# Hybrid decoder layer on one core: the low weight parts of the per-head products made on Pool instead of VectorE

## Chip, cores and metric

One NeuronCore of a Trainium2 chip runs the whole kernel. The metric is the device time of one execution in microseconds (us). The names of the engines are those of the profile: PE is TensorE (matmul), DVE is VectorE, ACT is ScalarE, POOL is GpSimd, SP is SyncE, which here only issues DMAs.

## What is computed

A hybrid decoder layer over 512 tokens of width 2048, in float32: an attention branch with forget gates (8 heads of 128) and an RWKV-7 branch (16 heads of 64, handled in 8 pairs), each gated, merged, projected and normalised.

```python
h = _rmsnorm(x, norm_gain)
u = h @ w_in                                  # 2048 x 12488
q, k, v, z_a, f_logit = _split(u_fox, ...)    # 4 x 1024 + 8 columns
o_a = _fox_attention(q, k, v, log_f) * silu(z_a)
r, kr, vr, z_b, w_down, a_down = _split(_token_shift(u_rwkv), ...)
y = _rwkv7_scan(r, decay, k, v, kk, kk * a)   # S = S*w + (S@-kk) b^T + v k^T per token
o_b = (groupnorm(y) + bonus) * silu(z_b)
m = sigmoid(g_a) * (o_a @ w_proj_fox) + sigmoid(g_b) * (o_b @ w_proj_rwkv)
out = _rmsnorm(x + m @ w_out, final_norm_gain)
```

## The kernel before

Every large product is done in three matmuls of a short float format: the operand is split into a high part (rounded) and a low part (the rest), and high x high, low x high and high x low are added up in PSUM. The activations' parts hhi and hlo are made once and stay in SBUF. The weights stream through.

A weight tile of 2048 x 128 is cut into four pieces of 128 x 512 values (256 KB). Each piece goes through four steps. SP issues its load into one of four raw buffers (`load_raw`, L236, the DMA on L239). ACT makes the high part whi by a copy that rounds (L266). Another engine makes the low part wlo = raw - whi (L267, and L263 for the first four pieces). PE uses the piece in twelve matmuls of 512 columns (`product`, L278, through `mm`, L127). There are four buffers each of whi and wlo. `next_piece` (L242) hands out piece i and writes down the loads up to piece i+4 and the splits up to piece i+2, so PE works some pieces behind the splits. A raw buffer is loaded again only when the wlo of the piece in it has been made; SP waits for that on its own queue, in the order of the program.

The pieces have names: ad for one LoRA input, k, r, z, v for the RWKV pairs, fq, fk, fv, fz for the attention heads, g for the gates, p for the projections, o for the output. The first letter decides in the changed line.

Time falls into three parts. Up to about 40 us the input is normalised and transposed. From 40 to about 990 us (the heads' stage) the products k, r, z, v of eight RWKV pairs and fq, fk, fv, fz of eight heads run as one main stream on PE, and the rest of the heads' work is woven between them. After that come gates, projections and the output product, a steady stream of matmuls. PE's and SP's instructions stand in the order of the program (`manual_schedule`, L154): the main stream advances a clock that counts PE's work alone, and a worker (`rwkv_front`, `rwkv_back`, `rwkv_chain`, `fox_head`) gets its next step when the clock has passed the delay of its last one (LAG, L52). The order on DVE, ACT and POOL is chosen by the framework when the program is built, by priority and an estimate of when operands are ready; `high_priority(offset=HW)` (L265) puts the splits ahead of what stands up to 150 instructions before them. At run time each engine works through its queue strictly in order.

Of the workers' steps the argument needs these. In `rwkv_back` DVE inverts small triangular blocks by 31 steps of a multiply (Wt, L641 through the helper at L482, both operands in SBUF) and a reduction (W, L642), one after the other; I call this the substitution loop. The attention heads' softmax stands among its last steps on DVE, and ACT's exponent (pr, L798) waits for the row maximum that DVE makes (fst, L796, L797). The loop's result goes out by SP to DRAM and back (w_d, L646 to L654), DVE transposes it (A, L658) and PE multiplies with it (gp, L675). `shift` (L443 to L448) takes an RWKV product out of PSUM by ACT and DVE, which frees one of the two PSUM banks of the main stream. In `rwkv_front` POOL makes two steps: a (L532) and kn = kn * a (L547, seen at L482), and DVE's split of rkk (L552, seen at L426) writes a buffer that this POOL step reads. POOL also copies AV (L705), clears parts of SV (L594) and issues the DMAs that store ob_d and oa_d (L771, L834).

Of the kernel before, what the change touches and what calls it, by code (L numbers as in the profile page):

```python
# [9 lines left out]
F32 = mybir.dt.float32  # L10
F32R = mybir.dt.float32r
AF = mybir.ActivationFunctionType
ALU = mybir.AluOpType
# [42 lines left out]
def hybrid_layer(  # L56
# [7 lines left out]
    V, S, G, PE = nc.vector, nc.scalar, nc.gpsimd, nc.tensor  # L64
# [177 lines left out]
    def next_piece():  # L242


        i = used[0]
        used[0] += 1
        while len(raws) < min(i + (RAWS + 1 if i > 3 else 4), len(pieces)):
            raws.append(load_raw(*pieces[len(raws)]))
        split_pieces(i + (3 if i > 3 else 1))
        got = parts[i]  # L250
        parts[i] = None
        return got

    def split_pieces(n):
        while len(parts) < min(n, len(pieces)):
            j = len(parts)
            name, srcs, nk, M = pieces[j]
            raw = raws[j]
            whi = wpool.tile([P, nk, M], F32R, tag="whi", bufs=4, name=f"whi_{name}")
            wlo = wpool.tile([P, nk, M], F32R, tag="wlo", bufs=4, name=f"wlo_{name}")  # L260
            if j < 4:
                G.tensor_copy(whi, raw)
                G.tensor_tensor(wlo, raw, whi.bitcast(F32), ALU.subtract)  # L263
            else:
                with tc.high_priority(offset=HW):  # L265
                    S.activation(whi, raw, AF.Copy)  # L266
                    V.tensor_tensor(wlo, raw, whi.bitcast(F32), ALU.subtract)  # L267
            parts.append((whi, wlo))


# [75 lines left out]
    for hf in range(2):  # L346
        t = slice(256 * hf, 256 * hf + 256)
        for j in range(0, KC + AHEAD, 2):
            if j < KC:
                turn(hf, j)  # L350
            if hf == 0 and j % 4 == 0 and j < KC:
                wd_w.append(next_piece())
                if j == 0:
                    for tb in range(2, 4):
                        for h2 in range(2):
                            load_x(nc.sync, tb, h2)
                    load_params()
            if hf == 0 and j in (SQ2, SQ3):
                norm_rows(2 if j == SQ2 else 3)
            if j < AHEAD:  # L360
                continue
            for kk in range(j - AHEAD, j - AHEAD + 2):
                whi, wlo = wd_w[kk // 4]
                mm(ps_wd[0:MW, t], whi[:, kk % 4, :], hhi[:, kk, t], start=(kk == 0), stop=False)
                mm(ps_wd[0:MW, t], whi[:, kk % 4, :], hlo[:, kk, t], start=False, stop=False)
                mm(ps_wd[0:MW, t], wlo[:, kk % 4, :], hhi[:, kk, t], start=False, stop=(kk == KC - 1))
            if hf == 1 and j - AHEAD in (4, 8, 12):
                split_pieces(4 + (j - AHEAD) // 4)
# [634 lines left out]
    for n in range(4):  # L1003
        pss = banks(n)
        for kk in range(KC if n < 3 else KC // 2):
            whi, wlo = next_piece()
# [55 lines left out]
```

## Time and profile before

| what | value |
|---|---|
| three runs | 1672.08, 1672.97, 1675.00 us; median 1672.97 us |
| the profiled execution's own time | 1676.68 us |
| its span, first to last instruction | 1674.8 us |
| busy over the span | PE 97%, DVE 57%, ACT 42%, POOL 5% |
| mean granted clock of PE | 0.993 |

Busy time alone does not tell what a change is worth. A busy PE can still have a queue that waited a moment before, and an engine that is half idle can be late at the few points where PE needs it. So the rows further down show first where PE stood still, and who released it, and then the durations of the operations that the change moves.

### The profile page before, as it was taken

The page shows a single profiled execution, that of the slowest core. Times are in us where ns is not written, and L with a number is a line of the kernel's source. Part 1 is how long each engine was busy: PE and PEld are TensorE (multiplying, and loading weights), DVE is VectorE, ACT ScalarE, POOL GpSimd, SP SyncE. Part 2 cuts the span into 40 slices and gives each one's busy share as a digit, 9 for nine tenths or more (in the row PEclk, how much of TensorE's full clock was granted, in tenths as well). Part 3 has the DMA queues.
Part 4 walks back from the last instruction along what each step waited for, and adds up shares of the span by engine and source line. Part 5 has one row for each costly group of instructions (what it writes and reads, how often), then busy time and mean ns, then how long its engine had stood idle before and what let it go on. Part 6 is the DMA issues. An engine that isn't in the chain of part 4 may idle for free.

```text
span 1674.8 us, 23424 instructions
## 1 busy us (share of the span) xinstructions
PE 1628.9 (97%) x8506; PEld 1332.3 (80%) x8506; DVE 958.0 (57%) x2005; ACT 710.4 (42%) x1453; POOL 83.6 (5%) x149
## 2 busy tenths in 40 slices
PE   6998998999999999999999999999999999999998
PEld 6887876778878778788788788888888888888886
DVE  6468587786877777678668454222224333353432
ACT  7544354474464464553744444222223222243322
POOL 3010001000000000010000000000000000001110
PEclk9999998999999999999999999999999999999999
DMA  5342423333333324334334244335334333343422
GB/s 167 97 107 69 105 61 90 98 87 86 90 96 98 99 70 111 86 78 104 85 86 115 76 123 118 95 98 148 94 96 148 97 95 98 98 160 117 138 83 101
DMA packets 287978, 170.24 MB, mean 102 GB/s; under 512 B 38790, under 2 KB 270830, under 8 KB 287222
## 3 DMA queue, kind: packets, MB, share of 16 engines
q1 hardware_dynamic: 284358, 156.13, 35.4%
q0 software_dynamic: 2064, 9.46, 1.5%
q10 hardware_dynamic: 1440, 3.15, 0.5%
q8 instruction: 67, 1.10, 0.3%
q14 instruction: 49, 0.40, 0.1%
HBM read 158.19 MB, written 10.50 MB: 101 GB/s over the span
## 4 chain that ended last, share of the span: by engine, by line
PE 83%; DVE 9%; ACT 3%; issue 2%; DMA 2%; SPq 1%; POOL 0%; DVEq 0%; ACTq 0%; POOLq 0%
PE u_g L135 20%; PE p L135 11%; PE o L135 10%; PE u_fq L135 6%; PE u_fk L135 5%; PE u_z L135 4%; PE u_fv L135 4%; PE u_k L135 4%; PE u_fz L135 4%; PE u_v L135 4%; PE u_r L135 2%; DVE Wt L482 2%; DVE W L642 1%; PE sc L135 1%; PE y L135 1%
## 5 line engine op out<-in xcount | busy, mean ns | idle before, releaser
L135 PE MATMUL u_g<-hhi,wlo_g 128*128 128x512 f32 x512 | 200.6, 392 | 0.0
L135 PE MATMUL u_g<-hhi,whi_g 128*128 128x512 f32 x512 | 200.4, 391 | 0.0
L135 PE MATMUL u_g<-hlo,whi_g 128*128 128x512 f32 x512 | 200.0, 391 | 0.0
L267 DVE TENSOR_TENSOR wlo_g<-raw_g,whi_g 128x512 fp32r<-128x512 f32 x128 | 88.4, 690 | 169.8 <-ACT whi_g L266 167.6
L266 ACT ACTIVATE whi_g<-raw_g 128x512 fp32r<-128x512 f32 x128 | 80.9, 632 | 228.1 <-PE u_g L135 115.1
L135 PEld LDWEIGHTS u_g<-hlo,whi_g 128*128 128x128 f32 x512 | 96.2, 188 | 20.3
L135 PEld LDWEIGHTS u_g<-hhi,wlo_g 128*128 128x128 f32 x512 | 96.2, 188 | 20.2
L135 PEld LDWEIGHTS u_g<-hhi,whi_g 128*128 128x128 f32 x512 | 96.2, 188 | 19.7
L482 DVE TENSOR_TENSOR Wt<-W,Lt 128x16 f32<-128x16 f32 (+30 forms) x248 | 101.0, 407 | 5.6
L267 DVE TENSOR_TENSOR wlo_p<-raw_p,whi_p 128x512 fp32r<-128x512 f32 x64 | 44.3, 693 | 103.3 <-ACT whi_p L266 103.3
L135 PE MATMUL p<-ohi,whi_p 128*128 128x512 f32 x256 | 101.0, 394 | 0.0
L135 PE MATMUL p<-ohi,wlo_p 128*128 128x512 f32 x256 | 100.4, 392 | 0.0
L135 PE MATMUL p<-olo,whi_p 128*128 128x512 f32 x256 | 99.6, 389 | 0.0
L266 ACT ACTIVATE whi_p<-raw_p 128x512 fp32r<-128x512 f32 x64 | 40.4, 631 | 121.9 <-PE u_g L135 120.3
L135 PE MATMUL o<-whi_o,mhi 128*128 128x512 f32 x224 | 87.3, 390 | 0.1
L135 PE MATMUL o<-wlo_o,mhi 128*128 128x512 f32 x224 | 87.2, 389 | 0.0
L135 PE MATMUL o<-whi_o,mlo 128*128 128x512 f32 x224 | 87.1, 389 | 0.0
L267 DVE TENSOR_TENSOR wlo_o<-raw_o,whi_o 128x512 fp32r<-128x512 f32 x56 | 42.6, 762 | 76.2 <-ACT whi_o L266 75.9
L642 DVE TENSOR_REDUCE W<-Wt 128x8 f32<-128x16 f32 (+30 forms) x248 | 72.4, 292 | 5.6
L266 ACT ACTIVATE whi_o<-raw_o 128x512 fp32r<-128x512 f32 x56 | 35.3, 631 | 83.6 <-PE o L135 79.3
L135 PE MATMUL u_fq<-hhi,whi_fq 128*128 128x512 f32 x128 | 53.7, 419 | 5.2 <-DVE z L448 5.2
L719 ACT ACTIVATE pre<-SV,E 64x64 f32<-64x64 f32 x112 | 38.6, 345 | 46.3 <-DVE SV L732 45.4
(352 smaller groups left out, 3924.3 us busy)
## 6 DMA issues: line engine op xcount, KB each, us to landing
raw_g<-in_w_in_dram SPq DMA_DIRECT2D x128, 256.0 KB
raw_o<-in_w_out_dram SPq DMA_DIRECT2D x56, 256.0 KB
raw_k<-in_w_in_dram SPq DMA_DIRECT2D x32, 256.0 KB
raw_r<-in_w_in_dram SPq DMA_DIRECT2D x32, 256.0 KB
raw_z<-in_w_in_dram SPq DMA_DIRECT2D x32, 256.0 KB
raw_v<-in_w_in_dram SPq DMA_DIRECT2D x32, 256.0 KB
raw_fq<-in_w_in_dram SPq DMA_DIRECT2D x32, 256.0 KB
raw_fk<-in_w_in_dram SPq DMA_DIRECT2D x32, 256.0 KB
```

What stands on the lines that cost most here:

```text
L135: PE.matmul(out, lhsT=lhsT, rhs=rhs, start=start, stop=stop, **kw)
L266: S.activation(whi, raw, AF.Copy)
L267: V.tensor_tensor(wlo, raw, whi.bitcast(F32), ALU.subtract)
L482: eng.tensor_tensor(o, a, b, op)
L642: V.tensor_reduce(W[:, :, i], tmp[:, :, 0:i + 1], AX.X, ALU.add)
L719: S.activation(pre[hs[q]], SV[hs[q], c, q, :], AF.Copy, scale=E1[hs[q], c, CH:CH + 1])
```

## The change

For pieces whose name begins with k, r, z, v or f, the subtraction that makes the low part is given to POOL (`G`) instead of DVE (`V`). These are the 256 pieces of the eight RWKV pairs and the eight heads. The four pieces of ad, and those of g, p and o, stay on DVE. Nothing else is edited; the orders on DVE, ACT and POOL are chosen anew when the program is built.

```diff
@@ -264,7 +264,7 @@
             else:
                 with tc.high_priority(offset=HW):
                     S.activation(whi, raw, AF.Copy)
-                    V.tensor_tensor(wlo, raw, whi.bitcast(F32), ALU.subtract)
+                    (G if name[0] in "krzvf" else V).tensor_tensor(wlo, raw, whi.bitcast(F32), ALU.subtract)
             parts.append((whi, wlo))
```

## Rows read from the trace of the kernel before

**Rows 1.** Busy time: stretch, length, PE, PEld, DVE, ACT, POOL, clock, DMA, GB/s
```profile
40.00:990.00 950.00, 925.16 (x5353) 751.59 (x5352) 690.13 (x1557) 473.55 (x1017) 47.79 (x71) 0.99 0.36 90
```

**Rows 2.** Waits of PE: tile and line, releaser, us in total, times, longest
```profile
PE gp L135 <- DVE A L658: 6.7, 2, 6.6
...
PE u_fq L135 <- DVE z L448: 5.2, 2, 4.5
PE bt L139 <- ACT BT L667: 3.3, 2, 1.7
...
PE st L135 <- ACT AV L725: 1.5, 3, 0.7
```

**Rows 3.** Timeline of PE at the two long waits: start, us, [idle before]
```profile
146.53 0.77 PE L135 MATMUL u_fq<-hhi,whi_fq 128*128 128x512 f32 x1 [4.54 <-DVE z L448]
147.09 0.63 PE L135 MATMUL u_fq<-hlo,whi_fq 128*128 128x512 f32 x1
147.52 0.63 PE L135 MATMUL u_fq<-hhi,wlo_fq 128*128 128x512 f32 x1
...
269.82 0.31 PE L135 MATMUL gp<-A,G 32*32 32x32 f32 x2 [6.59 <-DVE A L658]
```

**Rows 4.** Timelines of ACT, DVE and PE behind the seventh loop
```profile
796.07 0.40 ACT L798 ACTIVATE pr<-pr,fst 128x128 f32<-128x128 f32 x1 [4.91 <-DVE fst L797]
...
797.61 0.69 DVE L267 TENSOR_TENSOR wlo_r<-raw_r,whi_r 128x512 fp32r<-128x512 f32 x1 [0.36 <-PE u_r L135]
...
800.39 0.39 PE L135 MATMUL u_r<-hlo,whi_r 128*128 128x512 f32 x1
800.62 0.39 PE L135 MATMUL u_r<-hhi,wlo_r 128*128 128x512 f32 x1
```

**Rows 5.** The stretch behind the second wait, columns as in rows 1
```profile
270.00:275.00 5.00, 4.85 (x42) 3.89 (x41) 4.06 (x7) 1.60 (x3) 0.00 (x0) 0.54 0.06 16
```

**Rows 6.** Line 267: ns min/median/max, first and last start
```profile
L267 DVE TENSOR_TENSOR wlo_k<-raw_k,whi_k x32: 629/683/694, 40.8 to 786.9; 128x512 fp32r<-128x512 f32 x32
...
L267 DVE TENSOR_TENSOR wlo_fz<-raw_fz,whi_fz x32: 627/684/696, 178.7 to 982.7; 128x512 fp32r<-128x512 f32 x32
```

**Rows 7.** Waits of DVE as in rows 2, one line before low parts
```profile
DVE wlo_fv L267 <- ACT whi_fv L266: 15.8, 12, 4.5
```

**Rows 8.** Timeline of POOL: three of the eight kn steps
```profile
140.51 1.84 POOL L482 TENSOR_TENSOR kn<-kn,a 128x512 f32<-128x512 f32 x1 [5.99 <-DVE AR L545]
...
266.55 2.15 POOL L482 TENSOR_TENSOR kn<-kn,a 128x512 f32<-128x512 f32 x1 [5.33 <-DVE AR L545]
...
495.11 1.29 POOL L482 TENSOR_TENSOR kn<-kn,a 128x512 f32<-128x512 f32 x1 [5.13 <-DVE AR L545]
```

**Rows 9.** POOL groups: line, shapes, count, busy us and mean ns, idle before
```profile
L263 POOL TENSOR_TENSOR wlo_wd<-raw_wd,whi_wd 128x416 fp32r<-128x416 f32 x4 | 4.5, 1126 | 0.2
```

**Rows 10.** Timeline of DVE beside the first two kn steps
```profile
141.14 0.27 DVE L642 TENSOR_REDUCE W<-Wt 128x8 f32<-128x112 f32 x1
141.32 1.59 DVE L482 TENSOR_TENSOR AR<-r,E 128x512 f32<-128x512 f32 x1
...
263.22 0.63 DVE L482 TENSOR_TENSOR AR<-r,E 128x512 f32<-128x512 f32 x1
...
266.29 1.29 DVE L267 TENSOR_TENSOR wlo_fq<-raw_fq,whi_fq 128x512 fp32r<-128x512 f32 x2
268.73 0.69 DVE L426 TENSOR_TENSOR rlo<-rkk,rhi 128x512 fp32r<-128x512 f32 x1 [1.16 <-POOL kn L482]
```

**Rows 11.** Timeline of DVE in the output stage, beside four POOL multiplies
```profile
1537.87 3.47 DVE L267 TENSOR_TENSOR wlo_o<-raw_o,whi_o 128x512 fp32r<-128x512 f32 x2
```

**Rows 12.** Sums over eight loop stretches: all engines; Wt alone; line 267 alone
```profile
sum 303.00, PE 297.64 PEld 243.95 DVE 280.81 ACT 124.18 POOL 11.28; mean PE 37.21 PEld 30.49 DVE 35.10 ACT 15.52 POOL 1.41
...
sum 303.00, DVE 173.12; mean DVE 21.64
...
sum 303.00, DVE 60.46; mean DVE 7.56
```

## The prediction, made before the changed kernel was run

> **What bounds the kernel now.** I read the profile in three steps. First the busy time of the stage that the change touches: of the 950 us between 40 and 990 us PE is busy for 925.2, DVE for 690 and POOL for 48 [rows 1]. So PE sets the time, and all that any edit of DVE or POOL can give is what PE loses: 24.8 us of idle time, and a little clock. Second the list of PE's waits, which says who ended that idle time [rows 2]. Two sites are DVE's: 6.7 us in which gp waits for the transposed result of a substitution loop, and 5.2 us in which the main stream waits until a product has been taken out of PSUM. Five smaller lines, 11.7 us together, were ended by ACT (the first and the last of them are shown). No wait of PE for a low part is listed. Third the timeline at the two DVE sites [rows 3]: the waits are 4.54 us before 146.53 and 6.59 us before 269.82. Behind each of them PE runs slower for a while. After the first, matmuls start 0.43 us apart instead of 0.23 [rows 3, 4], twelve of them until 151.4 us, some 2.4 us. After the second, the granted clock is 0.54 over five microseconds, so mostly the lower level of 1.2 GHz instead of 2.4, which is worth 5 x 0.46 = 2.3 us [rows 5]. What both have in common is that PE stood idle before. The ceiling of a gain is therefore 24.8 + 2.4 + 2.3 = 29.5 us.
>
> **Removed from DVE.** The 256 subtractions take a median of 0.68 to 0.69 us (eight names of 32 each, the first and the last shown) [rows 6], 256 x 0.69 = 177 us of DVE's 690. With them goes idle time in which DVE, in the order of its queue, waits until ACT has made a high part (15.8 us for fv alone, 4.5 at the longest [rows 7]). This is off PE's path nearly everywhere.
>
> **Added to POOL.** The price of one on POOL is not in the trace. The nearest rows are the kn multiply of the same size and input type, 1.29 us when nothing disturbs it and up to 2.15 us beside DVE [rows 8], and the subtraction of 128 x 416 at 1.13 us [rows 9]. I take 1.29 as clean value, and bounds of 1.13 and 2.15. 256 x 1.29 = 330 us, up to 550: POOL goes from 48 to 380 or 600 of 950 us. PE eats a piece in no less than 12 x 0.23 = 2.7 us [rows 4], so POOL keeps up at either bound. The latency grows by 1.29 - 0.69 = 0.6 us, at most 1.5. PE has that to spare: I paired each low part with its first matmul, and between them lie 9 us in the median of the 256, and 2.3 us at the tightest, 798.30 to 800.62 [rows 4]. Cost on PE's path: nothing, as long as POOL's queue isn't held up. The ACT step before, the load and the other splits stay as they are.
>
> **Collisions.** At 140.51 POOL's kn and DVE overlap. DVE's AR multiply, with two inputs in SBUF, took 1.59 us, while the same instruction at 263.22 took 0.63 and a reduction with one input in the same overlap took its usual 0.27 [rows 10]. So a DVE instruction with two SBUF inputs that meets a running POOL one loses up to 0.96 us. Low parts beside POOL multiplies in the output stage took 3.47 / 2 = 1.74, a loss of 1.05 [rows 11]. It works the other way too: two DVE subtractions in a row at 266.29 were not slowed, and kn took 2.15 [rows 8, 10]. The Trainium skill says this as a rule (SBUF — State Buffer, § Who interferes with whom): a VectorE instruction with two SBUF inputs contends with a GpSimd instruction that reads SBUF, and whichever starts first holds the shared ports for its whole length. The rows above agree where the DVE instruction reads twice. By that rule alone, if each moved piece held DVE up whole, DVE would lose 256 x (1.29 - 0.69) = 154 us; the case in which this decides is rival 3. Bounds for the loss of DVE per moved piece: 0 and 1.05 us. In a substitution loop a two-input multiply comes in every step, with only a reduction between. The eight loops, 303 us together, hold 60.5 us of low parts [rows 12], some 88 pieces; there I take 0.9 each, 79 us for 60.5 removed: each loop gets about 2.3 us longer, not shorter. Outside, many DVE instructions read PSUM or have one input, and I take 0.25, nearer to the lower end, for the other 168: 42 us for 116 removed, a relief of 74 us.
>
> **What reaches PE.** Site one: from 128.6 to 145.7 us DVE has a loop and the front of the next pair mixed, and seven low parts among them: 4.8 us out, 7 x 0.5 = 3.5 in, so PE waits 1.3 us less (between 4.54 less and 2.6 more). Site two: six low parts from 247 to 267 us, 4.1 out, 3.0 in. DVE there also waits 1.16 us for POOL's kn before it can go on to A [rows 10]; kn may now stand behind a low part, up to 1.3 us, and I take 0.3. Sum: 0.8 us less (between 6.59 less and 3.5 more). Clock behind both: if the slow stretch shrinks with the wait, 29% of 2.4 and 12% of 2.3 us, 1.0. The ACT-ended waits of 11.7 us are steps that pass between DVE and ACT. Outside the loops DVE loses 74 of 409 us of busy time (690 less 281 in the loops [rows 1, 12]), 18%; I take a little over a fifth, 2.6 us (between 0 and 11.7). At the tightest loop, 2.3 us for the loop and 0.6 for the step are 2.9 against a slack of 2.3: 0.6 us more. **POOL's other steps** are a and kn (which, but for site two, feed steps that LAG puts 20 and 5 us of PE's work later), AV, the clears of SV and 16 DMA issues whose data is read in the next stage: each waits for one low part more, 1.3 to 2.2 us, nothing on the path. **SP** holds each raw load until the low part in its buffer is made. The loads get 0.6 us later, and with them the loops' DMAs that stand behind them in the queue; the same slack covers that. Total: 1.3 + 0.8 + 1.0 + 2.6 - 0.6 = 5.1 us less. Against the profiled execution's own time that is 1676.7 - 5.1 = 1671.6; it is 3.7 us above the median of the runs, so 1673.0 - 5.1 = **1667.9 us**.
>
> **Rivals.** (1) It comes out even: the collisions give back what was removed, the waits move elsewhere and stay at 24.8 us. For it: the sums at both sites are differences of 4 and 3 us. Against: 74 us of relief outside the loops. Time 1670 to 1676, about 1672.5. (2) The relief is whole: with no low part in its queue DVE reaches both sites in time, and the clock holds. 6.7 + 5.2 + 2.4 + 2.3 = 16.6 us [rows 2, 3, 5], 1656.4. For it: both sites lie where DVE has no idle time; against: kn and two-input work are dense there. (3) Slower, by the collisions in the loops. Place: ACT's queue behind a loop's end. The softmax of a head stands among the loop's last steps on DVE; ACT waits 4.91 us for it, the high part of r stands behind it on ACT, and the low part of 797.61 is ready only 2.3 us before use [rows 4]. Two other loops leave 3.5 and 3.7 us. A loop with eleven low parts at 1.05 instead of 0.69 is 4 us longer, and the POOL step itself is 0.6 to 1.5 us later: 4.6 to 5.5 us against 2.3, 3.5 and 3.7 gives waits of 2.3 to 3.2, 1.1 to 2.0 and 0.9 to 1.8. With 2 us more at site one and half-clock stretches behind, 8 to 10 us: about 1682. It decides from a loop that is 1.7 us longer. The loops are my weakest number: I put them at 2.3, just past it. (4) Slower, by POOL's order: a low part stands behind a DMA issue or a copy that waits for DVE, whose time the order was built on an estimate. On DVE's queue such a wait reaches 4.5 us today [rows 7]. Where one exceeds the slack, PE waits, perhaps 5 us in all: 1678. That the change does nothing is excluded: POOL will have 256 more instructions.
>
> **How the numbers follow.** A measurement of this kernel can tell about 0.2%, 3.3 us, from no change. Forecast 0.32 (its own range 1663 to 1669.6), rival 2 0.10, so faster 0.42; rival 1, same, 0.31; rival 3 0.15 and rival 4 0.12, slower 0.27. For 8 in 10 I cut about half of rival 2 below 1657 and the upper part of rival 3 above 1682.
>
> **What would show it.** In the changed profile: 256 low parts at POOL, 1.3 to 1.6 us each; DVE busy for 570 to 650 us between 40 and 990; loop stretches one to four microseconds longer, though they lost 7.6 us of other work; reductions of their old length, and two-input multiplies up to 1 us longer when POOL overlaps. PE's waits for A and z shorter but there; no wait of PE for a low part. Rival 3 would show as a longer wait of ACT for the softmax and of PE for whi or wlo of r behind a loop; rival 4 as PE waiting for POOL. I am wrong if the loops get shorter (collisions cost less than 0.69), or if PE's idle time moves to a site that is not in the list today.

## The result, and the profile after

The changed kernel takes 1718.02 us (median of four runs, 1717.34 to 1720.07) against 1673.99 us of the kernel before beside it: a ratio of 1.0265, with a 95% interval of 1.0247 to 1.0282. It is 44 us slower; the forecast was 5 us faster, with a range that ended at 1682. The profiled execution took 1717.69 us, 41.0 more than that of before, and all of this lies in the heads' stage, which ends at 1031 us instead of 990. Its busy times, with the columns of [rows 1]:

```profile
40.00:1031.00 991.00, 934.38 (x5352) 752.13 (x5351) 638.86 (x1301) 474.03 (x1019) 389.69 (x328) 0.99 0.34 87
```

DVE has less to do than before (639 instead of 690 us) and POOL much more (390 instead of 48), as the change wants it. But PE's idle time went from 24.8 to 56.6 us, and its busy time rose by 9.2 us. The waits of PE, as in [rows 2], show where; the first line is one from the kernel before that [rows 2] does not show, the others are of the changed kernel:

```profile
PE sa L135 <- ACT zt L715: 2.7, 6, 0.7
...
PE sa L135 <- ACT zt L715: 13.9, 14, 1.7
...
PE u_r L135 <- DVE fz L844: 7.0, 4, 2.9
...
PE st L135 <- ACT AV L725: 4.7, 7, 1.8
PE fpt L139 <- ACT BT L667: 3.8, 1, 3.8
...
PE u_fv L135 <- DVE fql L426: 3.5, 1, 3.5
PE gp L135 <- ACT fpT L809: 2.9, 2, 1.5
...
PE u_fq L135 <- DVE z L448: 1.2, 1, 1.2
...
PE u_r L135 <- POOL wlo_r L267: 0.6, 1, 0.6
```

The two long waits of [rows 2] are relieved: gp no longer waits for A, and u_fq waits 1.2 us for z instead of 5.2. In their place stand many waits of one to four microseconds at steps that hardly waited before: sa for zt (2.7 us before), u_r for the taking out of fz (none before), st for AV (1.5 before). The last row, 0.6 us, is the only wait for a moved low part that this list names.

What happened on DVE is seen in two groups of its instructions (busy us, mean ns; the kernel before first, then the changed one), and in a low part of POOL (ns min/median/max):

```profile
L482 DVE TENSOR_TENSOR Wt<-W,Lt 128x16 f32<-128x16 f32 (+30 forms) x248 | 101.0, 407 | 5.6
...
L642 DVE TENSOR_REDUCE W<-Wt 128x8 f32<-128x16 f32 (+30 forms) x248 | 72.4, 292 | 5.6
```

```profile
L482 DVE TENSOR_TENSOR Wt<-W,Lt 128x16 f32<-128x16 f32 (+30 forms) x248 | 161.6, 652 | 7.0
...
L642 DVE TENSOR_REDUCE W<-Wt 128x8 f32<-128x16 f32 (+30 forms) x248 | 72.6, 293 | 7.1
```

```profile
L267 POOL TENSOR_TENSOR wlo_fv<-raw_fv,whi_fv x32: 1267/1292/1342, 159.6 to 1009.8; 128x512 fp32r<-128x512 f32 x32
```

The multiplies of the substitution loops (two inputs in SBUF) took 101.0 us before and take 161.6 now, while the reductions (one input) kept their 292 ns. The added 60.6 us are as much as the low parts that left the loops. POOL's step is hardly touched: its median is the 1.29 us that I had taken as the clean price. One meeting, step by step, DVE above and POOL below:

```profile
574.76 1.46 DVE L482 TENSOR_TENSOR Wt<-W,Lt 128x184 f32<-128x184 f32 x1
576.25 0.35 DVE L642 TENSOR_REDUCE W<-Wt 128x8 f32<-128x184 f32 x1
576.63 0.53 DVE L482 TENSOR_TENSOR Wt<-W,Lt 128x192 f32<-128x192 f32 x1
...
577.59 1.38 DVE L482 TENSOR_TENSOR Wt<-W,Lt 128x200 f32<-128x200 f32 x1
```

```profile
574.56 1.30 POOL L267 TENSOR_TENSOR wlo_k<-raw_k,whi_k 128x512 fp32r<-128x512 f32 x1 [1.43 <-ACT whi_k L266]
577.28 1.29 POOL L267 TENSOR_TENSOR wlo_r<-raw_r,whi_r 128x512 fp32r<-128x512 f32 x1 [1.42 <-ACT whi_r L266]
```

The multiply at 574.76 begins 0.20 us behind the low part of k and ends 0.36 us behind its end; the next one, with a little more to do, takes 0.53; the one after that meets the low part of r and takes 1.38. Each of the 248 multiplies can be compared with the same step in the kernel before: 66 of them begin while a low part runs on POOL and carry 54.0 of the 60.6 us, and in 61 of the 66 the added time is what is left of that low part, less 0.14 us, within 0.06. The multiplies that begin while any instruction runs on POOL are 77, and they carry the whole 60.6 us. DVE waits to POOL's end. The Trainium skill (SBUF — State Buffer, § Who interferes with whom) says that of a VectorE instruction with two SBUF inputs and a GpSimd instruction that reads SBUF the one that starts first keeps the shared ports for its whole length. The 61 of 66 agree.

How such a delay reaches PE is seen behind the loop that ends at 828.8 us, on DVE, PE and ACT, and in the busy times of the stretch after it:

```profile
828.80 0.68 DVE L844 SCALAR_TENSOR_TENSOR fz<-fz,u_fz 128x512 f32<-128x512 f32 x1
...
829.62 0.47 PE L135 MATMUL u_r<-hhi,whi_r 128*128 128x512 f32 x1 [2.88 <-DVE fz L844]
...
831.02 0.40 ACT L798 ACTIVATE pr<-pr,fst 128x128 f32<-128x128 f32 x1 [9.73 <-DVE fst L797]
...
830.40:833.80 3.40, 3.40 (x9) 2.62 (x8) 1.04 (x7) 2.78 (x9) 0.00 (x0) 0.52 0.10 25
```

DVE takes fz out of PSUM only when the loop is done, and u_r needs that bank: PE stands for 2.88 us. ACT has waited 9.73 us for the softmax behind the same loop (4.91 in [rows 4]). Behind the idle time the granted clock of PE is 0.52 for 3.4 us, near the lower of its levels of 1.2 and 2.4 GHz, as in [rows 3, 5]. There are six such stretches of 3.4 us now; before there were three, of 6.8, 10.2 and 3.4 us. They last as long in all, so the clock is not what made the time longer, and the 9.2 us more of busy time are not the clock. About half of them is the way busy time is counted: PE now stops 50 times for more than 0.15 us instead of 23, and the last matmul before a stop counts with its whole 0.39 us, where a following one starts after 0.23 [rows 4]; 27 x 0.16 = 4.3 us, an estimate. What the rest is I could not separate.

### The profile page after: what moved, and what is told of

Its sections match the earlier page's. It is cut to its first block, busy times and chain, and to the rows that moved or that the text cites. A ratio compares the mean times of both kernels' runs of the same rounds, so it can differ in the third digit from the quotient of the medians.

```text
span 1715.9 us, 23417 instructions
## 1 busy us (share of the span) xinstructions
PE 1637.8 (95%) x8506; PEld 1332.5 (78%) x8506; DVE 906.2 (53%) x1749; ACT 710.4 (41%) x1455; POOL 424.9 (25%) x405
## 4 chain that ended last, share of the span: by engine, by line
PE 71%; DVE 20%; issue 3%; ACT 2%; DMA 2%; SPq 1%; POOL 0%; DVEq 0%; ACTq 0%; POOLq 0%
PE u_g L135 19%; PE p L135 10%; PE o L135 10%; DVE Wt L482 8%; PE u_fq L135 4%; PE u_fk L135 4%; DVE W L642 3%; PE u_z L135 3%; PE u_r L135 3%; PE u_k L135 3%; PE u_fv L135 3%; PE u_v L135 2%; PE u_fz L135 2%; DVE kn L540 1%; PE sc L135 1%
## 5 line engine op out<-in xcount | busy, mean ns | idle before, releaser
L482 DVE TENSOR_TENSOR Wt<-W,Lt 128x16 f32<-128x16 f32 (+30 forms) x248 | 161.6, 652 | 7.0
L135 PE MATMUL p<-ohi,whi_p 128*128 128x512 f32 x256 | 101.0, 394 | 0.0
L267 POOL TENSOR_TENSOR wlo_r<-raw_r,whi_r 128x512 fp32r<-128x512 f32 x32 | 42.5, 1334 | 89.7 <-ACT whi_r L266 72.5
L267 POOL TENSOR_TENSOR wlo_fq<-raw_fq,whi_fq 128x512 fp32r<-128x512 f32 x32 | 44.2, 1381 | 75.7 <-ACT whi_fq L266 73.8
```

The source lines that it names most:

```text
L135: PE.matmul(out, lhsT=lhsT, rhs=rhs, start=start, stop=stop, **kw)
L267: (G if name[0] in "krzvf" else V).tensor_tensor(wlo, raw, whi.bitcast(F32), ALU.subtract)
L482: eng.tensor_tensor(o, a, b, op)
```

## Experiments

Two theories stood at first. Theory A: the collisions make DVE's chains longer. Theory B: the order on DVE, chosen anew without the low parts, puts steps behind a loop's end (fz stands ahead of step 25 to 28 of the loops before, behind step 31 of five loops in the changed kernel) and is bad by itself. Rival 4 of the prediction, POOL's own order, came in later. Below, the pieces of a loop are named by its pair ("unit" in the expectations), and a "stretch" is the time on PE from the start of one product to the start of the next. The edits are shortened to the words that differ, and ratios are taken against runs of the kernel before made beside each.

**Zeros instead of the subtraction.**

```diff
-(G if name[0] in "krzvf" else V).tensor_tensor(wlo, raw, whi, subtract)
+G.memset(wlo, 0.0) if name[0] in "krzvf" else V.tensor_tensor(wlo, raw, whi, subtract)
```

> POOL fills the 256 low parts with zeros instead of subtracting, so it writes the same tiles and reads nothing; the low part of these weights is left out of the products. The order on DVE and ACT stays that of the changed kernel but for six and eight lines. Theory A (collisions: POOL's reading holds up DVE's multiplies of the substitution loops): the 248 Wt steps fall from 161.6 us back to about 101, PE's idle time from 78 to 46 us or less, time 1655 to 1675. Theory B (order: what the new order puts behind a loop's end is late, whatever the length of the steps): Wt falls too if collisions are real, but fz still stands behind the loop and PE still waits there; time 1700 to 1720. Half of each: about 1690. If POOL's writing holds the ports as well, Wt stays at 150 to 160 and the time near 1718.

Measured: 1648.62 us, ratio 0.9845 (0.9829 to 0.9862). Its multiplies and PE's wait for zt:

```profile
L482 DVE TENSOR_TENSOR Wt<-W,Lt 128x16 f32<-128x16 f32 (+30 forms) x248 | 101.4, 409 | 7.0
```

```profile
PE sa L135 <- ACT zt L715: 4.1, 7, 1.0
```

With the order of the changed kernel, but nothing read by POOL, the multiplies are back at 101.4 us, no wait for fz is left, and the time is 26 us below the kernel before. The time lies even below the range that I had written for theory A (1655 to 1675). So the new order alone does no harm, and theory B falls in this form. A POOL instruction that only writes holds up nothing: 47 multiplies begin while one runs, and lose 0.2 us together. The Trainium skill (SBUF — State Buffer, § Who interferes with whom) says that a GpSimd instruction that only writes SBUF does not contend, and the 47 agree.

**The subtraction done on both engines.** The order of the kernel before, with collisions.

```diff
 V.tensor_tensor(wlo, raw, whi, subtract)
+if name[0] in "krzvf": G.tensor_tensor(raw, raw, whi, subtract)
```

> The kernel before, whose low parts stay on DVE; POOL makes the same subtraction once more into the raw buffer, whose values nobody reads again. DVE's order is that of the kernel before but for two lines. PE waits for nothing of POOL's; the raw buffers come free some 1.3 to 2 us later. Theory A: Wt goes to 150 to 165 us although the order is kept, and DVE carries 177 us of low parts besides, so the time is at least that of the changed kernel: 1715 to 1750. Theory B: about 1673 to 1680, since the order is the old one. Half of each: about 1695.

Measured: 1753.66 us, ratio 1.0475 (1.046 to 1.0491).

```profile
L482 DVE TENSOR_TENSOR Wt<-W,Lt 128x16 f32<-128x16 f32 (+30 forms) x248 | 146.3, 590 | 5.6
```

The old order is kept and 79 us are lost: collisions do their harm without the new order. Theory A holds; its number for the multiplies (150 or more) was a little high and its time (up to 1750) a little low. Not all of the 79 us need be the collisions': the raw buffers come free later in this run, and ACT waits 10.0 us for loads of r (0.4 in the kernel before).

**Only the pieces outside the loops, and only those inside.**

```diff
-(G if name[0] in "krzvf" else V).tensor_tensor(...)
+(G if name[0] in "krzvf" and (name not in LOOP) else V).tensor_tensor(...)   # the other: name in LOOP
```

> Of the 256 pieces only the 161 that don't lie in or next to a substitution loop go to POOL; the other 95 stay on DVE. DVE's order keeps fz ahead of the loops' last steps, as before. The account of the prediction (outside the loops a moved piece costs DVE 0.25 us and gives 0.69): Wt stays near 101 to 108 us, DVE is relieved by some 70 us outside, time 1664 to 1672. Collisions with the chain's steps and evacuations outside the loops (PE's new wait of 13.9 us for zt): 1680 to 1700.

> The counterpart: only the 95 pieces in or next to a substitution loop go to POOL. If the loops carry the loss (theories A and B alike): 1705 to 1718, Wt near 155 to 162 us. If the loss comes from all over: 1685 to 1700. The two losses of this run and of the one that moves the other 161 should add up to about 44 us if the pieces act one by one.

Measured: 1689.51 us (ratio 1.0092, 1.0077 to 1.0107) for the 161 pieces outside, 1700.55 us (1.0158, 1.0143 to 1.0174) for the 95 inside. The losses, 15.0 and 26.0 us, add up to 41 of the 44: the pieces act nearly one by one. The 95 came out between the two ranges that I had written. My account for the pieces outside (1664 to 1672) is refuted. In that run the multiplies of the loops stay at 101.0 us, DVE's busy time over the span falls by 68 us, and yet PE loses. The place is the front of a pair, which runs while PE works on v. On DVE and POOL, then PE's waits:

```profile
375.06 1.03 DVE L486 TENSOR_TENSOR EK<-EK,k 128x512 f32<-128x512 f32 x1
376.01 0.94 DVE L544 RECIPROCAL kn<-kn 128x128 f32<-128x128 f32 x1
376.98 0.22 DVE L718 COPY zt<-z 64x64 f32<-64x64 f32 x1
377.12 1.62 DVE L546 SCALAR_TENSOR_TENSOR kn<-k,par,kn 128x512 f32<-128x512 f32 x1
...
381.92 1.73 DVE L430 TENSOR_TENSOR rlo<-rkk,rhi 128x512 fp32r<-128x512 f32 x1
...
386.39 0.22 DVE L718 COPY zt<-z 64x64 f32<-64x64 f32 x1
```

```profile
374.02 1.53 POOL L536 TENSOR_SCALAR a<-a 128x512 f32<-128x512 f32 x1
376.93 1.27 POOL L267 TENSOR_TENSOR wlo_v<-raw_v,whi_v 128x512 fp32r<-128x512 f32 x1 [1.38 <-ACT whi_v L266]
...
381.85 1.26 POOL L267 TENSOR_TENSOR wlo_fq<-raw_fq,whi_fq 128x512 fp32r<-128x512 f32 x1
...
377.49 0.32 PE L135 MATMUL sa<-zt,DT 128*128 128x64 f32 x1 [1.37 <-ACT zt L719]
...
386.90 0.43 PE L135 MATMUL sa<-zt,DT 128*128 128x64 f32 x2 [0.86 <-ACT zt L719]
```

The small copy zt, on which the chain of the pair before depends, stands in DVE's queue behind the front's long steps. Ahead of the second zt shown, kn and rlo each wait for a low part (1.62 and 1.73 us), and PE waits 0.86 us for it. Ahead of the first zt, EK takes 1.03 us beside POOL's own step a, as it does in the run with zeros. In the kernel before these steps took:

```profile
374.61 0.22 DVE L714 COPY zt<-z 64x64 f32<-64x64 f32 x1
374.75 0.68 DVE L482 TENSOR_TENSOR EK<-EK,k 128x512 f32<-128x512 f32 x1
...
376.92 0.75 DVE L542 SCALAR_TENSOR_TENSOR kn<-k,par,kn 128x512 f32<-128x512 f32 x1
...
382.50 0.67 DVE L426 TENSOR_TENSOR rlo<-rkk,rhi 128x512 fp32r<-128x512 f32 x1
```

There zt also stood ahead of EK, so the order has a part in the place of the wait. But the run with zeros has the later place of zt too, and its stretch of v of pair 3 takes 15.9 us, as in the kernel before, against 18.7 here. The loss needs the collisions.

**The pieces outside without v and fq.**

```diff
-... and (name not in LOOP)
+... and name[0] != "v" and name[:2] != "fq" and (name not in LOOP)
```

> Of the 161 pieces outside the loops those of v and fq stay on DVE as well; 110 go to POOL. In the run with all 161 most of the loss against the kernel before, some 10 of 15 us, lies in the stretch of u_v in units 3 to 7, where PE waits for zt while DVE makes the two-input steps of rwkv_front beside POOL's v and fq pieces. If that place is the cause: 1672 to 1680, PE's waits for zt back to 3 to 5 us. If the loss is spread evenly over the pieces: about 1685. If the relief of DVE is worth something by itself: under 1670.

Measured: 1680.44 us, ratio 1.0039 (1.0025 to 1.0052). PE's wait for zt, with all 161 and with these 110:

```profile
PE sa L135 <- ACT zt L719: 9.9, 11, 2.2
```

```profile
PE sa L135 <- ACT zt L719: 5.1, 7, 1.9
```

Nine of the 15 us are gone with 51 of the pieces, those that meet the front; an even spread would have given 1685. The place is shown. (The run also brings back the old order at the front; that the order alone is no cause rests on the run with zeros.) From the starts of the products on PE I also took the lengths of the stretches at both places (us; the loops of pairs 3 to 6 end beside k and r of pairs 4 to 7, and the stage ends here with the last product of the heads, some 3 us behind the windows used above):

| kernel | start of fk of head 1 | k and r of pairs 4 to 7 | v of pairs 3 to 7 | end of the stage |
|---|---|---|---|---|
| before | 285.1 | 114.1 | 79.5 | 992.9 |
| changed | 285.8 | 138.3 | 90.0 | 1034.0 |
| 161 pieces outside | 281.9 | 114.9 | 89.9 | 1004.9 |
| 95 pieces inside | 281.7 | 138.3 | 79.6 | 1019.1 |
| 110 pieces | 284.6 | 112.8 | 79.5 | 996.3 |
| zeros | 269.1 | 107.4 | 79.9 | 966.6 |

The loss behind the loops (24.2 us) comes from the pieces inside alone, that at v (10.5 us) from the pieces outside alone, and the two are 35 of the 41 us.

**One input, and shorter instructions.**

```diff
+G.tensor_copy(wlo, whi)                        # first run, in place of the subtraction
+for q in range(4): G.tensor_tensor(wlo[:, q], raw[:, q], whi[:, q], subtract)   # second run
```

> POOL copies the high part into the place of the low part instead of subtracting: one input from SBUF instead of two, the same tile written, and the wait for ACT's high part kept; the low part of these weights is wrong in the products. The order on DVE and ACT stays that of the changed kernel but for six and eight lines. If any reading of POOL holds the ports, Wt rises with the length of the copy: some 130 to 160 us, time 1685 to 1718. If only a second input collides, Wt stays near 101 us and the time near the 1649 us of the run with zeros; the wait for ACT's high part, which that run had taken away too, then costs nothing. Between the two, 1655 to 1665 with Wt near 101, the wait would be what cost.

> The changed kernel with each of the 256 subtractions on POOL cut in four of 128 x 128. If a POOL instruction holds the ports for its own length and lets DVE in at its end, a Wt step waits for a quarter of the time but meets four of them: the sum of Wt stays at 140 to 165 us and the time at 1705 to 1722, since DVE alternates with POOL. If a meeting costs a fixed amount, whatever the length, Wt rises far above 162 us and the time above 1740. If the length of the hold is what counts, and short holds mostly fall beside the reductions, Wt falls to 115 to 130 and the time to 1680 to 1695.

Measured: 1653.20 us (ratio 0.9874, 0.986 to 0.9887) with the copy, 1687.95 us (1.0081, 1.0067 to 1.0095) with quarters. The multiplies and one POOL group of each run, the copy first:

```profile
L482 DVE TENSOR_TENSOR Wt<-W,Lt 128x16 f32<-128x16 f32 (+30 forms) x248 | 109.4, 441 | 7.0
...
L267 POOL CAST wlo_fv<-whi_fv x32: 610/614/967, 157.7 to 945.4; 128x512 fp32r<-128x512 f32 x32
```

```profile
L482 DVE TENSOR_TENSOR Wt<-W,Lt 128x16 f32<-128x16 f32 (+30 forms) x248 | 132.6, 535 | 7.0
...
L267 POOL TENSOR_TENSOR wlo_fv<-raw_fv,whi_fv x128: 452/461/913, 157.7 to 980.7; 128x128 fp32r<-128x128 f32 x128
```

The copy holds up DVE too (in 53 of 56 meetings by what is left of it, less 0.14 us), only for a shorter time: it takes 0.61 us instead of 1.29. Four quarters take 1.84 us together, more than the whole, and still cost half as much: multiplies 31.6 us longer instead of 60.6, and 39 us of time above the run with zeros instead of 69 (13.6 us above the kernel before instead of 44). 138 multiplies begin while a quarter runs, twice as many as with whole pieces, but lose 0.23 us each in the mean instead of 0.82. So it is not POOL's work that costs, nor the latency of a low part, which is longest here, but the length of the single hold. I had put this outcome third, with 1680 to 1695. None of my three cases for the copy came: against the run with zeros Wt rose by 8 us and the time by 5.

**Longer loops without a collision.**

```diff
 V.tensor_reduce(W[:, :, i], tmp[:, :, 0:i + 1], AX.X, ALU.add)
+if i % 2: V.tensor_reduce(W[:, :, i], tmp[:, :, 0:i + 1], AX.X, ALU.add)
```

> The kernel before, low parts on DVE, with every second reduction of the substitution loops made twice: 16 more instructions of 0.29 us in each of eight loops, 4.6 us a loop, 37 us in all, without any collision, and known to the estimate from which the order is built. That order puts the taking out of fz at steps 21 to 24 of the loops instead of 25 to 28, and the softmax ahead of the last steps. In the changed kernel the loops of units 3 to 7 got 0.6 to 5.5 us longer, which the estimate did not know. If a longer loop is passed on to PE in any case, as it stands on DVE's chain: 1695 to 1715. If it costs only where the order does not expect it: 1673 to 1682. By the slack that the prediction read (2.3, 3.5 and 3.7 us at three loops, more at the others): 1677 to 1684.

> The changed kernel with every second reduction of the substitution loops made twice, as in the run with longer loops: 37 us more of DVE's work, which the estimate behind the order knows; the collisions, which it does not know, stay. The new order takes fz out at steps 25 to 29 of the loops in units 2 to 7 instead of behind them. If only the length of the loops counts, the two losses add: 1718 + 25 = 1743. If it counts that the loops take longer than the order was built for, the added work makes order and run agree better and costs little or nothing: 1705 to 1725, with less idle time of PE in the stretches of u_r in units 3 to 7 than in the changed kernel.

Measured: 1698.97 us, ratio 1.0147 (1.0133 to 1.0161), for the kernel before with it; 1741.90 us, 1.0405 (1.0387 to 1.0422), for the changed kernel with it. The same 37 us of work cost 25 us in the one and 24 in the other, though both orders knew of it: in sum the losses add (1743), and neither the sum by the prediction's slack (1677 to 1684) nor the theory that only unexpected length costs gives these times.

The places tell more. In the first run the loops of pairs 4 to 6 are 6.4 to 6.8 us longer than in the kernel before, and k and r of pairs 5 to 7, beside their ends, cost nothing (0.3 us less in all). In the run with the subtraction on both engines, collisions make the same loops 5.6 to 7.2 us longer, and these products cost 22.1 us more. The first run, whose order puts fz ahead, loses elsewhere: at fv of head 0 (6.9 us), fq of head 1 (4.1), z of pair 3 (8.2) and r of pair 4 (5.1), for the most part where PE waits for the loop's own result:

```profile
PE gp L135 <- DVE A L658: 21.0, 11, 9.6
```

Why known steps cost nothing at the late loops and collisions do, no run here separates.

**The stores off POOL's queue.** One delay in the changed kernel is of another kind; DVE above, POOL below:

```profile
449.67 5.04 DVE L482 TENSOR_TENSOR Wt<-W,Lt 128x200 f32<-128x200 f32 x1
```

```profile
448.73 0.56 POOL L771 DMA_DIRECT2D ob_d<-y  x1 [1.87 <-DVE W L642]
449.30 5.02 POOL L267 TENSOR_TENSOR wlo_k<-raw_k,whi_k 128x512 fp32r<-128x512 f32 x4
```

POOL's queue waited for y before the store, four low parts piled up behind it, and one multiply waited for all four.

```diff
-G.dma_start(ob_d[p], t2)
+stores.append([6, ob_d[p], t2])      # SP issues it six pieces later; second run: oa_d too
```

> The changed kernel with the store of each pair's result (ob_d) issued by SP, six pieces later in the program, instead of by POOL. Orders on PE, DVE and ACT stay (two lines of ACT differ). In the changed kernel POOL waited 1.9 us for y before the store at 448.73, four low parts of k piled up behind it, ran without a gap and held one Wt step for 5.04 us; four other stores have smaller piles. If POOL's order (rival 4 of the prediction) is a part of the loss: the step of 5.04 us goes, the stretch of u_r in unit 3 gets some 5 to 8 us shorter, 1705 to 1713. If each meeting costs what it costs wherever POOL's pieces run: 1715 to 1720.

> As the run before, and the heads' stores (oa_d) by SP too, so that POOL has no DMA issue between low parts; in the changed kernel it waits 2.2 to 6.5 us at these, with pieces of v and fq behind. If piles behind waits of POOL carry much of the loss: 1695 to 1708. If they are one place only: as the run before, within 3 us. If the meetings carry it: 1715 to 1720.

> The control: the kernel before with both kinds of store by SP. No low part stands behind a store on POOL there, so 1671 to 1677 by every theory; another time would mean that the way of the store counts by itself and has to be taken off the two runs before.

Measured: 1714.08 us (ratio 1.0236, 1.0214 to 1.0258), 1714.31 us (1.0235, 1.0219 to 1.025), and 1679.45 us (1.0019, 1.0009 to 1.0028) for the control. The multiply of 5 us is gone (the longest is now 1.69), and 4 us with it, which is no more than the first of these runs scatters (1711 to 1719); the second is clear of it. Moving the second kind of store adds nothing. The control is 0.2% slower, so the way of the store costs something itself, and POOL's order may be worth up to some 8 us; it is a small part of the 44 either way. With the stores by SP, low parts still follow each other without a gap, but now DVE gets in between them. DVE, then POOL (two low parts in each row):

```profile
455.42 1.15 DVE L492 TENSOR_TENSOR Wt<-W,Lt 128x232 f32<-128x232 f32 x1
...
457.03 1.17 DVE L492 TENSOR_TENSOR Wt<-W,Lt 128x240 f32<-128x240 f32 x1
```

```profile
454.70 3.04 POOL L277 TENSOR_TENSOR wlo_k<-raw_k,whi_k 128x512 fp32r<-128x512 f32 x2 [5.07 <-ACT whi_k L276]
457.70 3.31 POOL L277 TENSOR_TENSOR wlo_r<-raw_r,whi_r 128x512 fp32r<-128x512 f32 x2
```

Each of the two multiplies is done 0.4 to 0.5 us behind the end of one low part, and the next low part then takes 1.65 to 1.67 us instead of 1.29.

**Only where PE waits for DVE.** The experiments point to few pieces, at the two long waits, in short instructions.

```diff
-g = name[0] in "krzvf"
+g = name.split("_")[0] in ("v1", "fq0", "v2", "fq1")     # 16 pieces; second run: each in quarters; third: 60 pieces in quarters
```

> The kernel before with only 16 pieces on POOL, v and fq of the units ahead of the two long waits of PE for DVE (v of the pairs 1 and 2, fq of the heads 0 and 1). If the relief works where DVE's queue is what PE waits for, the waits of 4.5 us (u_fq for z) and 6.6 us (gp for A) shrink by 5 to 9 us together, and half-clock stretches behind them with them: 1663 to 1670, better than both kernels. If the collisions at the front take it back there too: 1671 to 1677.

> The run with 16 pieces (v of the pairs 1 and 2, fq of the heads 0 and 1), each cut in quarters. If the length of a hold is what costs, the 4.9 us that the run with whole pieces lost in the stretch of u_v of pair 2 shrink to 1 or 2: 1663 to 1667, 3 to 5 us below that run. If the number of instructions counts, no better than it: 1668 to 1671.

> Only pieces up to fq of head 1 go to POOL, cut in quarters, without k and r of pair 2 (60 of the 256); all later ones stay on DVE. In the run with all pieces in quarters the start of fk of head 1 came 8.8 us earlier than in the kernel before, and the loss came later. Short holds and only the stretch with the two waits for DVE: 1662 to 1667. If the gain is used up by later waits: 1668 to 1673.

Measured: 1669.31 us (ratio 0.9972, 0.996 to 0.9984), 1664.95 us (0.995, 0.9936 to 0.9963) with quarters, and 1668.38 us (0.9968, 0.9956 to 0.9979) for the 60 pieces in quarters. All three beat both kernels. More pieces were worse than 16, the case for which I had written that later waits use the gain up; and the stretch of v of pair 2 still lost 3.5 us with quarters (4.9 with whole pieces, 1 to 2 expected). In the best run the two long waits are gone; u_fq starts without a wait, 4.7 us earlier than in [rows 3]:

```profile
141.56 0.39 PE L135 MATMUL u_v<-hhi,wlo_v 128*128 128x512 f32 x1
141.79 0.47 PE L135 MATMUL u_fq<-hhi,whi_fq 128*128 128x512 f32 x1
```

## Why the prediction was wrong

**What bounds the kernel** was right: PE's idle time is what moved, and the ceiling of a gain, 29.5 us, was not passed even by the run with zeros (26 us), in which PE is idle for 7 us in the stage instead of 24.8.

**The prices on POOL and DVE** were right, or too high. POOL's step costs the 1.29 us assumed. In the loops I had 79 us of collisions and 60.6 were measured. For the other steps of DVE I had 42; without low parts and multiplies, the durations of its instructions in the first 1100 us add up to 38 us more than before. DVE's busy time, 639 us, lies in the range given. The loops became 1.5 us longer on average (297.1 to 309.4 us in all), less than the 2.3 forecast; but the first three hardly changed or got shorter, and four of the last five got 2.2 to 4.0 us longer, the tightest one 4.0.

**The two sites** did better than forecast. The wait for z shrank by 3.3 us at u_fq (1.3 forecast) and the wait for A went altogether (0.8 forecast). But waits for fql (3.5 us at u_fv) and in the chain gave it back in the products between: at the start of fk of head 1 nothing is left (285.1 before, 285.8 after).

**"What reaches PE" is the step that failed**, in two of its terms. The first is the 2.6 us that I credited at the ACT-ended waits: DVE's load outside the loops falls by 18%, so the waits shrink by a fifth. They grew; zt alone went from 2.7 to 13.9 us. The second is the 0.6 us charged behind the tightest loop, because three loops left 2.3 to 3.7 us of slack and the others more. With the lengths that these three loops really got (4.0, 2.2 and 4.0 us more) the same reckoning gives 1.1 + 0 + 2.3 = 3.4 us; measured are 14.8 us at k and r of pairs 5 to 7, and 24.2 with pair 4. So it is not the loops' length that was wrong but the slack. It was measured on one route, from the softmax over ACT's queue to the low part of r, in the order of the kernel before. The delay took others: the PSUM bank of fz, which the new order frees only behind the loop, the softmax's own matmuls, fql. Both terms count DVE's time without asking on which step it falls. Set against DVE's busy time over the span, the runs give (differences in us):

| from, to | DVE busy | time | time per us of DVE |
|---|---|---|---|
| before, zeros (low parts away) | -150.0 | -25.9 | 0.17 |
| zeros, changed (collisions) | +98.2 | +69.4 | 0.71 |
| zeros, copy | +16.0 | +4.6 | 0.29 |
| zeros, quarters | +45.8 | +39.3 | 0.86 |
| before, both engines | +85.7 | +79.1 | 0.92 |
| before, longer loops | +26.2 | +25.1 | 0.96 |
| changed, longer loops | +28.6 | +23.9 | 0.84 |

A low part on DVE has 9 us until its use; taking it away gives PE a sixth of its time, and could not give much more, as PE had only 29.5 us to win. A collision falls on the steps of a loop or of a front, each of which the next one waits for; it takes from PE seven tenths or more of its time, unless it is as small as with the copy. The added reductions do the same (0.65 to 0.96: of their 37 us, 26 and 29 show as busy time). So 256 pieces that leave DVE with less work leave PE with 26 us less and 69 us more.

**Rival 3** had the right cause and one of the two places, the end of a loop, but a size of 8 to 10 us, and a chance of 0.15. It was to decide from a loop 1.7 us longer, and four loops are; my own forecast of 2.3 was already past that, and I charged 0.6 us for it. The second place, zt behind the front's steps, was in no rival; its 2.7 us were among the 11.7 that I expected to shrink. **Rival 4** (POOL's order, 5 us) is there with some 4 us (up to 8). **Rival 2** (whole relief, 1656) is what the run with zeros shows, with more than I gave it. The order that the change makes anew, which I took as unchanged, is not a cause by itself: it costs nothing without collisions, and the old order loses with collisions too. It does decide where the loss falls.

**What would show it:** low parts at 1.29 us, reductions unchanged, multiplies about 1 us longer (but for the one behind four low parts), shorter waits for A and z came as written. The loops did so only in part. What I named as the sign of an error came too: PE's idle time went to sites that were not in the list.

Open remains how the loss splits among the routes behind a loop: the waits of the list were not taken away one by one. Open, too, is how much of it each order could have hidden.

## What to carry to other kernels

Ask of a moved operation not how much time its old engine gains, but on which steps its new engine's contention falls, and who waits for these. Work with slack is cheap where it is, and small delays in the steps of a serial chain were passed on for the most part here, even where each wait looked harmless in the profile before. A slack read from one trace belongs to the order of that trace. If an engine with shared access is to help, give it short instructions, and only at the few places where the profile shows the bottleneck engine waiting.

## What the hardware showed that I had not expected

Whether DVE gets in between two POOL instructions that follow without a gap depends on the place. In the run with quarters 82 of 84 such multiplies were done shortly behind the end of the first quarter (0.29 us in the median), and the next quarter took 0.66 us instead of 0.46; the run with the stores by SP shows the same with whole low parts. But in three piles, each behind a store issued by POOL, it was not let in: four low parts in a row held one multiply for 5.04 us, and in the run with quarters sixteen in a row, 6.73 us, held one for 6.76 and four held one for 1.76. What keeps it out there, no run shows. So DVE loses to a running POOL instruction, and POOL only where its next one meets a DVE instruction that has waited: POOL's median stayed at 1.29 us while 66 multiplies waited. Three POOL instructions of 128 x 512 that differ in what they read cost DVE's multiplies very different amounts: the subtraction (1.29 us) 60.6 us in all, the copy (0.61 us) 8.4, the fill with zeros (0.53 us), which reads nothing, 0.4. And a subtraction of 128 x 128 takes 0.46 us, so cutting one in four makes it 0.55 us longer on POOL and still costs DVE's multiplies half as much.
